# A two-layer attention model on one core: the rope of the keys done in place in the projection's PSUM bank, and their high and low parts taken from there

## The chip, the core and the metric

The kernel runs on one core of a Trainium2 chip. Its time is that of one execution on the device in microseconds (us). The engines are PE (TensorE matmuls; PEld is its weight load), DVE (VectorE), ACT (ScalarE), POOL (GpSimd) and SP (SyncE, which issues the DMAs). L211 is line 211 of the kernel before.

## The reference

512 tokens of width 1024 pass two layers. Each adds an attention and a feed forward with a causal convolution, each behind an RMS norm. Layer 0's attention (16 query heads, 4 key-value groups of width 64) has three branches with gates: compressed keys, selected blocks, and a window. Layer 1 (2 key-value groups) attends within a band of 128 tokens with a sink. Where keys are concerned, cut:

```python
def rope(x, pos):
    ...
    x1, x2 = xf[..., :half], xf[..., half:]
    return jnp.concatenate([x1 * cos - x2 * sin, x2 * cos + x1 * sin], axis=-1)

# layer 0
q, kc, vc, ks, vs, kw, vw, gl = jnp.split(h @ w_in, split_idx, axis=-1)
ks = rope(ks.reshape(b, s, g_n, dh), pos)
kw = rope(kw.reshape(b, s, g_n, dh), pos)
# layer 1
k, v = jnp.split(rms_norm(h, kv_norm) @ w_kv, 2, axis=-1)
k = rope(k.reshape(b, s, B_KV_HEADS, HEAD_DIM), jnp.arange(s))
```

All is float32.

## The kernel before

Every float32 product is made as three matmuls of rounded parts: x is hi + lo, and hi*hi, hi*lo and lo*hi are summed (mm3, L102 to L104). So each operand is copied to its high part on ACT and the low part is subtracted on DVE or POOL; for weights that is wh (L116) and wl (L117), and the strings W_A and W_B say weight by weight which of DVE and POOL subtracts. SPLIT_A and SPLIT_B say it for other operands by a key; 'kcat' stands for the low part of the keys.

The tokens are four tiles of 128. The PSUM banks are in three pools: pss (two tiles of two banks), pst (three of one bank) and psv (one). A projection to 256 columns of keys and values puts, for one token tile, two heads of keys (128 columns) beside two of values (128 columns). It comes out of project_steps, a pst tile per token tile (groups 1 to 3 of layer 0), or project_outer, all four token tiles in the two banks of one pss tile (group 0, and layer 1).

evac_kv takes such a token tile away. rope multiplies the keys by the cosines (L211, rope1) and the swapped halves by the sines (L214, rope2, two instructions) on DVE, from PSUM to SBUF, and sums the two (L215) to the SBUF tile kn. split_v scales the values and splits them from PSUM: high part on ACT (L268), low part on DVE (L269), both into Vg (VB in layer 1). cat_k copies kn to its high part on ACT (L198) and subtracts for the low part (L199), on DVE in layer 0 and on POOL in layer 1, into kcat. stack_k, called later, transposes kcat on PE (L282) to a pst tile, which ACT copies to Kg (KB in layer 1; L287). Queries take another way: rope to Qg or Qb (L211, L214, the sum L215 on DVE or POOL), a scaled copy qd on POOL (L291), transposes on PE (L300), then qh on ACT (L302) and ql on DVE (L303).

The attention goes by quads, four heads of a token tile: scores on PE into pss (L713, L714), their maximum nmx on DVE (L725), exponentials on ACT (L736), the gates prm or prl on POOL (L743), transposes (L310) to pth (ACT, L314) and ptl (DVE, L315), products with Vg into psv (L764, L765), then otmp on ACT (L327) and the sums osum on DVE (L331). The projections of the next group run among the quads of a group: weave and place put their steps at places given by tables, and a scheduler then sets the order of instructions on each engine by their dependences. Two engines that touch one PSUM bank are kept in order by semaphores, by bank, whichever columns they touch.

Of the kernel before, what the change touches and what calls it, by code (L numbers as in the profile page):

```python
# [33 lines left out]
# which of Pool (P) and DVE (V) takes a subtraction or sum that either can: the low parts of the weights, in  # L34
# order (layer 0, layer 1), and of other operands
W_A = "VVPVVVVVPPPPPPPPPVVVPPVVVVVPVVVVPPPPPPPPPPPVPPPVPVPPPPPPPPP"
W_B = "PVVVPVPVVPVPVPPVPPPPPPPPPPPPPPPPPPPPPPPP"
SPLIT_A = {'out': 'P', 'rope': 'S', 'ropek': 'V', 'kcat': 'V', 'cmp': 'V', 'stack': 'P', 'every': 99}
SPLIT_B = {'out': 'P', 'rope': 'S', 'kcat': 'P', 'stack': 'P'}
# where the steps of the attention phases go among one another, in units of quads (four heads of a token tile)  # L40
# [10 lines left out]
# where the norm of the first half of the tokens goes in the products of the second half  # L51
# [4 lines left out]
# columns of the constant table  # L56
# [5 lines left out]
# columns of the mask table  # L62
# [10 lines left out]
def hybrid_kernel(ctx, tc, t):  # L73
# [73 lines left out]
    def warm_exp(dep):  # L147
        # the exponential's table, loaded ahead of its first use
        act(small.tile([P, 1], F32, name="warm", bufs=1), dep, AF.Exp, scale=0.0)

# [12 lines left out]
    def token_scale(ssq=None):  # L163
        """1 / rms of each token, [P, NT] with tokens on partitions."""
# [10 lines left out]
    def spread_scale(r_nat):  # L175
        """The same along the free axis, on every partition, in PSUM."""
# [11 lines left out]
    def weave(*lists):  # L188
        """Emit lists of steps side by side, each in its own order; (steps, first, last) places one."""
# [28 lines left out]
    # in four steps, one token tile and one bank each  # L218
# [22 lines left out]
    # or in four steps along the contraction, two token tiles to a bank  # L241
# [19 lines left out]

    def rope_tables(r_nat, tab):
        for i in range(NT):
            nc.vector.tensor_scalar(tab[:, i], rope_t[:, i], r_nat[:, i:i + 1], None, op0=OP.mult)

    def split_v(dst, src, r):
        # dst [P, g, 2, 64] f32r, src [P, g, 64] in PSUM
# [4 lines left out]
    def cat_k(pool, k, n):  # L272
        # k [P, n, 64] natural -> the same as hi|lo
# [4 lines left out]
    def stack_k(dst, kc, n):  # L278
        # -> dst [(hi|lo, d), n, P]
# [26 lines left out]
    def probs_t(pool, blocks, way="V"):  # L306
        # four [P, P] blocks -> split [key, head, query]
# [851 lines left out]
```

## Time and profile before

| | |
|---|---|
| runs, median | 1300.07 us (1298.43 to 1300.89, 3 runs) |
| the profiled execution's own time: its span | 1298.1 us |
| PE busy | 1251.8 us, 96% |
| DVE busy | 831.9 us, 64% |
| ACT busy | 629.9 us, 49% |
| POOL busy | 661.4 us, 51% |

Busy shares are over the whole span: layer 0's attention takes about the first 350 us, layer 1's lies between about 750 and 900 us, and the rest is the feed forwards. An engine's idle time matters only where PE waits for it. A row's duration includes time in which an instruction is held back.

### The profile page before, as it was taken

The numbers are of one execution on the slowest core, as the hardware profiler recorded it, in microseconds if no ns is written. First come the engines' busy times: TensorE is split into PE (matmuls) and PEld (weight loads), VectorE is DVE, ScalarE is ACT, GpSimd is POOL, SyncE is SP. The second block draws the span as 40 slices with busy tenths as digits, with TensorE's granted clock in tenths as the row PEclk, the third lists the DMA queues.
The fourth block names the chain that finished last, engine by engine and source line by source line (L and its number), as shares of the span: only waits on it lengthen the run. The fifth ranks groups of instructions, "written<-read, shape, count | busy, mean of one in ns | idle before, by whom it ended". The sixth has DMA issues, their size and how long they took to land.

```text
span 1298.1 us, 17657 instructions
## 1 busy us (share of the span) xinstructions
PE 1251.8 (96%) x6539; PEld 1041.9 (80%) x6539; DVE 831.9 (64%) x1331; ACT 629.9 (49%) x1278; POOL 661.4 (51%) x536
## 2 busy tenths in 40 slices
PE   8988999999999999999999999899999999999997
PEld 7887787878778888888888898777788888888886
DVE  5877868787458775047776458775497730577712
ACT  4555867777454443124444347665454421344332
POOL 6425767766484444444445446664644444444452
PEclk9998999999999999999999999999999999999999
DMA  5342011121122222222222131111222222232221
GB/s 187 115 155 80 1 34 34 34 98 34 33 97 91 88 97 98 97 88 91 98 98 97 49 115 33 34 65 49 98 82 98 98 97 95 84 97 98 97 82 65
DMA packets 34085, 106.45 MB, mean 82 GB/s; under 512 B 4048, under 2 KB 6608, under 8 KB 34000
## 3 DMA queue, kind: packets, MB, share of 16 engines
q1 hardware_dynamic: 34000, 105.34, 24.1%
q8 instruction: 51, 0.84, 0.3%
q14 instruction: 34, 0.28, 0.1%
HBM read 103.23 MB, written 2.10 MB: 81 GB/s over the span
## 4 chain that ended last, share of the span: by engine, by line
PE 86%; DVE 8%; ACT 3%; issue 1%; DMA 1%; SPq 0%; POOL 0%; DVEq 0%; ACTq 0%; POOLq 0%
PE pss L103 14%; PE pss L104 14%; PE pss L102 14%; PE pst L102 10%; PE pst L104 10%; PE pst L103 10%; PE pst L310 3%; DVE s L185 2%; PE psv L765 1%; PE pss L713 1%; PE psv L764 1%; PE pss L714 1%; PE pst L300 1%; DVE s L347 1%; DVE nmx L725 1%
## 5 line engine op out<-in xcount | busy, mean ns | idle before, releaser
L117 POOL TENSOR_TENSOR wl<-wr,wh 128x1024 fp32r<-128x1024 f32 (+1 forms) x173 | 406.3, 2350 | 437.8 <-ACT wh L116 434.5
L116 ACT CAST wh<-wr 128x1024 fp32r<-128x1024 f32 (+2 forms) x201 | 197.7, 985 | 347.6 <-issue 173.1
L103 PE MATMUL pss<-s,wh 128*128 128x512 f32 x736 | 292.0, 397 | 3.8 <-DVE s L185 3.8
L102 PE MATMUL pss<-s,wh 128*128 128x512 f32 x736 | 291.3, 396 | 2.3 <-ACT s L198 2.1
L104 PE MATMUL pss<-s,wl 128*128 128x512 f32 x736 | 290.8, 396 | 0.0
L103 PEld LDWEIGHTS pss<-s,wh 128*128 128x128 f32 x736 | 138.3, 188 | 39.5 <-DVE s L185 6.2
L102 PEld LDWEIGHTS pss<-s,wh 128*128 128x128 f32 x736 | 138.1, 188 | 37.1 <-ACT s L198 3.0
L104 PEld LDWEIGHTS pss<-s,wl 128*128 128x128 f32 x736 | 138.3, 188 | 32.6
L104 PE MATMUL pst<-actv,wl 128*128 128x512 f32 (+1 forms) x363 | 141.0, 389 | 0.0
L103 PE MATMUL pst<-actv,wh 128*128 128x512 f32 (+1 forms) x363 | 140.7, 388 | 0.0
L102 PE MATMUL pst<-actv,wh 128*128 128x512 f32 (+1 forms) x363 | 140.3, 386 | 0.0
L415 DVE SCALAR_TENSOR_TENSOR cv<-u,convp,cv 128x512 f32<-128x512 f32 x88 | 123.2, 1439 | 13.4 <-ACT cv L414 13.4
L199 DVE TENSOR_TENSOR actv<-sa,actv 128x512 fp32r<-128x512 f32 x44 | 101.6, 2312 | 30.7 <-ACT actv L198 30.5
L443 DVE TENSOR_TENSOR s<-s,pst 128x512 f32<-128x512 f32 x31 | 21.3, 687 | 155.4 <-PE pst L104 155.4
L412 DVE TENSOR_TENSOR u<-pss,R 128x512 f32<-128x512 f32 x84 | 54.1, 686 | 64.5 <-PE pss L104 64.5
L420 ACT ACTIVATE sa<-cv 128x512 f32<-128x512 f32 x44 | 27.9, 634 | 123.1 <-DVE cv L417 123.0
L103 PEld LDWEIGHTS pst<-actv,wh 128*128 128x128 f32 x363 | 68.4, 188 | 15.2
L102 PEld LDWEIGHTS pst<-actv,wh 128*128 128x128 f32 x363 | 68.4, 188 | 14.8
L104 PEld LDWEIGHTS pst<-actv,wl 128*128 128x128 f32 x363 | 68.4, 188 | 13.9
L314 ACT CAST pth<-pst 128x512 fp32r<-128x512 f32 x92 | 53.7, 594 | 35.0 <-PE pst L310 30.9
L315 DVE TENSOR_TENSOR ptl<-pst,pth 128x512 fp32r<-128x512 f32 x92 | 62.2, 683 | 12.8 <-ACT pth L314 11.9
L414 ACT ACTIVATE cv<-u,convp 128x512 f32<-128x512 f32 x88 | 66.6, 807 | 2.2 <-DVE u L412 2.2
(242 smaller groups left out, 2634.4 us busy)
## 6 DMA issues: line engine op xcount, KB each, us to landing
wr<-fin SPq DMA_DIRECT2D x88, 512.0 KB, 3.3
wr<-fout SPq DMA_DIRECT2D x44, 512.0 KB, 3.2
wr<-wg SPq DMA_DIRECT2D x10, 512.0 KB, 3.3
wr<-cw SPq DMA_DIRECT2D x8, 512.0 KB, 3.4
wr<-woA SPq DMA_DIRECT2D x8, 512.0 KB, 3.8
wr<-woB SPq DMA_DIRECT2D x8, 512.0 KB, 3.3
wr<-wqb SPq DMA_DIRECT2D x6, 512.0 KB, 3.3
s<-xT SPq DMA_DIRECT2D x8, 256.0 KB, 5.3
```

Of the source, the lines that this page charges most:

```text
L102: mm(out, ah, bh, start=start, stop=False)
L103: mm(out, ah, bl, start=False, stop=False)
L104: mm(out, al, bh, start=False, stop=stop)
L116: nc.scalar.copy(hi[:, :n], raw[:, :n])
L117: engines[next(pick["w"], "P")].tensor_sub(lo[:, :n], raw[:, :n], hi[:, :n].bitcast(F32))
L199: engines[pick["split"][name] if name else "V"].tensor_sub(lo, src, hi.bitcast(F32))
L310: pe_tr(ps[:, r * P:(r + 1) * P], blocks[r], ident)
L314: nc.scalar.copy(ph, ps)
L315: nc.vector.tensor_sub(pl, ps, ph.bitcast(F32))
L412: nc.vector.tensor_mul(u[:, s, 2:], src, norm["R"])
L414: act(cv[:, s], u[:, s, 2:], AF.Identity, bias=par[:, 3:4], scale=par[:, 2:3])
L415: nc.vector.scalar_tensor_tensor(cv[:, s], u[:, s, 1:S + 1], par[:, 1:2], cv[:, s], op0=OP.mult, op1=OP.add)
```

## The change

rope_in_place multiplies the swapped halves by the sines into the SBUF tile rope2, then multiplies the keys by the cosines in place, PSUM to the same PSUM, and adds rope2 to them, again in place. cat_k then reads the keys from PSUM, on ACT and on DVE, and only after it split_v takes the values. The tile kn and the key 'ropek' go; in layer 1 'kcat' moves from POOL to DVE. The queries keep rope. The rest of the diff takes comments away.

```diff
-SPLIT_A = {'out': 'P', 'rope': 'S', 'ropek': 'V', 'kcat': 'V', 'cmp': 'V', 'stack': 'P', 'every': 99}
-SPLIT_B = {'out': 'P', 'rope': 'S', 'kcat': 'P', 'stack': 'P'}
+SPLIT_A = {'out': 'P', 'rope': 'S', 'kcat': 'V', 'cmp': 'V', 'stack': 'P', 'every': 99}
+SPLIT_B = {'out': 'P', 'rope': 'S', 'kcat': 'V', 'stack': 'P'}
...
+    def rope_in_place(pool, src, tab, n):
+        t2 = pool.tile([P, n, HD], F32, name="rope2", bufs=2)
+        for a, b in ((0, HALF), (HALF, 0)):
+            ss = tab[:, 1, a:a + HALF].unsqueeze(1).to_broadcast([P, n, HALF])
+            nc.vector.tensor_mul(t2[:, :, a:a + HALF], src[:, :, b:b + HALF], ss)
+        nc.vector.tensor_mul(src, src, tab[:, 0, :].unsqueeze(1).to_broadcast([P, n, HD]))
+        nc.vector.tensor_add(src, src, t2)
...
         def evac_kv(g):
             def evac(i, ps):
-                kn = pa.tile([P, 2, HD], F32, name="kn", bufs=2)
                 pv = ps[:, :256].rearrange("p (h d) -> p h d", d=HD)
-                rope(pa, kn, pv[:, 0:2], tab[:, i], 2, pick["split"]["ropek"] if g else "V")
+                rope_in_place(pa, pv[:, 0:2], tab[:, i], 2)
+                kcs[g, i] = cat_k(pa, pv[:, 0:2], 2)
                 split_v(V[g][:, i], pv[:, 2:4], r_nat[:, i:i + 1])
-                kcs[g, i] = cat_k(pa, kn, 2)
             return evac
...
         def evac_kv(i, ps):
-            kn = pb.tile([P, GB, HD], F32, name="kn", bufs=2)
             pv = ps.rearrange("p (h d) -> p h d", d=HD)
-            rope(pb, kn, pv[:, 0:GB], tab[:, i], GB)
+            rope_in_place(pb, pv[:, 0:GB], tab[:, i], GB)
+            kcs[i] = cat_k(pb, pv[:, 0:GB], GB)
             split_v(VB[:, i], pv[:, GB:2 * GB], r_nat[:, i:i + 1])
-            kcs[i] = cat_k(pb, kn, GB)
```

With the code the scheduler's order changes, in the two attentions alone. The changed kernel's line numbers are other ones: L267 is the half products, L268 the product in place, L269 the sum in place, L277 and L278 the values' parts, L291 stack_k's transposes, L296 its copy; L309, L311 and L312 are what L300, L302 and L303 were, L733, L340 and L747 what L725, L331 and L739 were.

First, DVE at the last key tile of layer 0's group 3, around 260 us in the trace of before. Before:

```order
L211 TENSOR_TENSOR rope_3497<-pst,tab 128x128
L214 TENSOR_TENSOR rope_3498<-pst,tab 128x2x32 x2
L215 TENSOR_TENSOR kn<-rope_3497,rope_3498 128x128
L269 SCALAR_TENSOR_TENSOR Vg<-pst,r_nat,Vg 128x2x64
L725 TENSOR_REDUCE nmx<-pss 128x2
L199 TENSOR_TENSOR kcat<-kn,kcat 128x2x64
L331 TENSOR_TENSOR osum<-psv,otmp 64x256 x2
```

The same stretch of DVE with the change:

```order
L267 TENSOR_TENSOR rope_3466<-pst,tab 128x2x32 x2
L268 TENSOR_TENSOR pst<-pst,tab 128x128
L269 TENSOR_TENSOR pst<-pst,rope_3466 128x128
L733 TENSOR_REDUCE nmx<-pss 128x2
L340 TENSOR_TENSOR osum<-psv,otmp 64x256 x2
L199 TENSOR_TENSOR kcat<-pst,kcat 128x2x64
L733 TENSOR_REDUCE nmx<-pss 128x2
L747 RECIPROCAL cf<-sums 128x2
L278 SCALAR_TENSOR_TENSOR Vg<-pst,r_nat,Vg 128x2x64
```

The low part kcat stands behind osum instead of ahead of it, and the values' low part Vg moves from the third place behind the products to the end.

Second, ACT where group 0's keys are put away at the start of the attention, around 91 to 97 us in the trace of before (prm is here a tile of the compression, ACT_TABLE_LOAD brings the table of the exponential). Before:

```order
L198 CAST kcat<-kn 128x2x64
L287 CAST KcT<-pst 128x128
L198 CAST kcat<-kn 128x2x64
L287 CAST Kg<-pst 128x256
L595 ACTIVATE prm<-psv 128x256
L116 CAST wh<-wr 128x1024
L149 ACT_TABLE_LOAD
L149 ACTIVATE warm<-prm 128x1
L287 CAST Kg<-pst 128x256
L302 CAST qh<-pst 128x512
L287 CAST Kg<-pst 128x256
```

The same stretch of ACT with the change:

```order
L277 ACTIVATE Vg<-pss,r_nat 128x2x64
L603 ACTIVATE prm<-psv 128x256
L116 CAST wh<-wr 128x1024
L149 ACT_TABLE_LOAD
L149 ACTIVATE warm<-prm 128x1
L296 CAST Kg<-pst 128x256
L198 CAST kcat<-pss 128x2x64
L311 CAST qh<-pst 128x512
L116 CAST wh<-wr 128x1024
L277 ACTIVATE Vg<-pss,r_nat 128x2x64
L296 CAST Kg<-pst 128x256
```

The last kcat of group 0 and the Vg behind it stand behind the table load; before, both kcat stood ahead of it.

Third, DVE at the start of layer 1's attention, around 758 to 769 us in the trace of before (rope<-pst and rope<-pss of 128x256 are queries, those of 128x128 keys). Before:

```order
L215 TENSOR_TENSOR kn<-rope_7538,rope_7539 128x128
L117 TENSOR_TENSOR wl<-wr,wh 128x1024
L269 SCALAR_TENSOR_TENSOR VB<-pss,r_nat,VB 128x2x64
L211 TENSOR_TENSOR rope_7556<-pss,tab 128x256
L214 TENSOR_TENSOR rope_7557<-pss,tab 128x4x32 x2
L215 TENSOR_TENSOR Qb<-rope_7556,rope_7557 128x256
L117 TENSOR_TENSOR wl<-wr,wh 128x1024
L211 TENSOR_TENSOR rope_7600<-pst,tab 128x256
L214 TENSOR_TENSOR rope_7601<-pst,tab 128x4x32 x2
L211 TENSOR_TENSOR rope_7610<-pss,tab 128x256
L214 TENSOR_TENSOR rope_7611<-pss,tab 128x4x32 x2
L215 TENSOR_TENSOR Qb<-rope_7610,rope_7611 128x256
```

The same stretch of DVE in layer 1 with the change:

```order
L199 TENSOR_TENSOR kcat<-pss,kcat 128x2x64
L211 TENSOR_TENSOR rope_7560<-pst,tab 128x256
L278 SCALAR_TENSOR_TENSOR VB<-pss,r_nat,VB 128x2x64
L267 TENSOR_TENSOR rope_7499<-pss,tab 128x2x32 x2
L214 TENSOR_TENSOR rope_7517<-pss,tab 128x4x32 x2
L268 TENSOR_TENSOR pss<-pss,tab 128x128
L215 TENSOR_TENSOR Qb<-rope_7516,rope_7517 128x256
L269 TENSOR_TENSOR pss<-pss,rope_7499 128x128
L214 TENSOR_TENSOR rope_7561<-pst,tab 128x4x32 x2
L211 TENSOR_TENSOR rope_7570<-pss,tab 128x256
L214 TENSOR_TENSOR rope_7571<-pss,tab 128x4x32 x2
L199 TENSOR_TENSOR kcat<-pss,kcat 128x2x64
```

Before, the last VB stands ahead of all query products. Now the query product out of pst stands ahead of the third VB, and the fourth token tile's rope and kcat lie among the queries' products.

## Rows read from the trace of the kernel before

**Rows 1.** The page, part 1: busy time of each engine, its share of the span, and its instructions.

```profile
PE 1251.8 (96%) x6539; PEld 1041.9 (80%) x6539; DVE 831.9 (64%) x1331; ACT 629.9 (49%) x1278; POOL 661.4 (51%) x536
```

**Rows 2.** The waits of PE over the whole span: tile and line that waited, engine, tile and line waited for, then microseconds in total, times, longest.

```profile
PE pst L282 <- DVE kcat L199: 3.9, 2, 2.1
...
PE pst L102 <- ACT Kg L287: 1.8, 2, 1.5
```

**Rows 3.** The view of the tile kn: duration in ns as min/median/max, then first and last start. L215 is the rope's sum, L199 the low part.

```profile
L215 DVE TENSOR_TENSOR kn<-rope,rope x20: 271/292/1878, 74.1 to 759.4; 128x128 f32<-128x128 f32 x20
...
L199 DVE TENSOR_TENSOR kcat<-kn,kcat x16: 266/289/2167, 75.9 to 263.6; 128x128 fp32r<-128x128 f32 x16
L199 POOL TENSOR_TENSOR kcat<-kn,kcat x4: 461/486/1367, 755.8 to 766.2; 128x128 fp32r<-128x128 f32 x4
```

**Rows 4.** Groups of instructions by line, with shapes kept apart: count, busy microseconds in all, mean ns of one, idle time before them. L211 and L214 are the products of the rope of one token tile's keys, L269 and L268 the two parts of its values.

```profile
L214 DVE TENSOR_TENSOR rope<-pst,tab 128x64 f32<-128x64 f32 x24 | 4.1, 214 | 0.0
...
L269 DVE SCALAR_TENSOR_TENSOR Vg<-pst,r_nat,Vg 128x128 fp32r<-128x128 f32 x12 | 4.1, 341 | 0.5 <-ACT Vg L268 0.4
...
L211 DVE TENSOR_TENSOR rope<-pst,tab 128x128 f32<-128x128 f32 x12 | 3.5, 288 | 5.0 <-PE pst L104 4.4 <-POOL wl L117 0.5
...
L268 ACT ACTIVATE Vg<-pst,r_nat 128x128 fp32r<-128x128 f32 x12 | 4.6, 382 | 7.1 <-DVE rope L214 7.1
```

**Rows 5.** The timeline around 200 us (last key tile of group 2), one row each of POOL, DVE and PE: start us, duration us (of all that a row counts together), engine, line, operation, tiles, count, and in brackets the idle time before it and what ended it. So are the columns in all groups from here on, but for the window in rows 6.

```profile
197.30 4.75 POOL L117 TENSOR_TENSOR wl<-wr,wh 128x1024 fp32r<-128x1024 f32 x2
...
200.02 2.17 DVE L199 TENSOR_TENSOR kcat<-kn,kcat 128x128 fp32r<-128x128 f32 x1
...
202.25 0.37 PE L282 MATMUL pst<-identr,kcat 128*128 128x128 f32 x2 [2.09 <-DVE kcat L199]
```

**Rows 6.** The timeline around 262 us (last key tile of group 3), of POOL, DVE, ACT and PE, and under it the window from 250 to 275 us: its length, busy time and instructions of PE, PEld, DVE, ACT and POOL, the granted clock of PE, the share of DMA, GB/s.

```profile
259.76 4.77 POOL L117 TENSOR_TENSOR wl<-wr,wh 128x1024 fp32r<-128x1024 f32 x2 [2.02 <-ACT wh L116]
...
260.62 1.69 DVE L215 TENSOR_TENSOR kn<-rope,rope 128x128 f32<-128x128 f32 x1
...
262.50 1.21 DVE L725 TENSOR_REDUCE nmx<-pss 128x2 f32<-128x1024 f32 x1
263.63 1.05 DVE L199 TENSOR_TENSOR kcat<-kn,kcat 128x128 fp32r<-128x128 f32 x1
264.60 0.84 DVE L331 TENSOR_TENSOR osum<-psv,otmp 64x256 f32<-64x256 f32 x2
...
262.94 0.58 ACT L327 COPY otmp<-psv 64x512 f32<-64x512 f32 x1
...
264.83 0.33 PE L282 MATMUL pst<-identr,kcat 128*128 128x128 f32 x2 [1.84 <-DVE kcat L199]
...
250.00:275.00 25.00, 22.40 (x149) 18.89 (x148) 20.26 (x45) 20.27 (x55) 18.11 (x20) 0.93 0.34 127
```

**Rows 7.** The timeline from 94 to 106 us (keys of group 0 put away, keys of group 1 projected), of ACT, DVE and PE.

```profile
94.74 1.28 ACT L149 ACT_TABLE_LOAD   x1
...
96.14 0.35 ACT L287 CAST Kg<-pst 128x256 fp32r<-128x256 f32 x1
...
100.32 0.37 ACT L268 ACTIVATE Vg<-pst,r_nat 128x128 fp32r<-128x128 f32 x1 [2.11 <-DVE rope L214]
...
99.88 0.34 DVE L214 TENSOR_TENSOR rope<-pst,tab 128x64 f32<-128x64 f32 x2
...
105.35 0.34 DVE L269 SCALAR_TENSOR_TENSOR Vg<-pst,r_nat,Vg 128x128 fp32r<-128x128 f32 x1
...
96.55 0.39 PE L102 MATMUL pst<-wh,s 128*128 128x256 f32 x1 [1.46 <-ACT Kg L287]
...
105.74 1.12 PE L300 MATMUL pst<-cst,qd 128*128 128x128 f32 x4 [0.81 <-DVE Vg L269]
```

**Rows 8.** The timeline from 766 to 770 us (start of layer 1's attention), of DVE, POOL and PE.

```profile
766.85 0.42 DVE L211 TENSOR_TENSOR rope<-pst,tab 128x256 f32<-128x256 f32 x1 [0.94 <-PE pst L104]
767.19 0.48 DVE L214 TENSOR_TENSOR rope<-pst,tab 128x128 f32<-128x128 f32 x2
767.58 0.41 DVE L211 TENSOR_TENSOR rope<-pss,tab 128x256 f32<-128x256 f32 x1
...
768.43 0.43 DVE L215 TENSOR_TENSOR Qb<-rope,rope 128x256 f32<-128x256 f32 x1
...
768.95 0.62 POOL L291 TENSOR_SCALAR qd<-Qb 128x512 f32<-128x512 f32 x1 [0.47 <-DVE Qb L215]
...
769.61 0.29 PE L282 MATMUL pst<-identr,kcat 128*128 128x128 f32 x2
769.74 0.62 PE L300 MATMUL pst<-cst,qd 128*128 128x128 f32 x4
```

**Rows 9.** The timeline around 111 and 249 us, of PE and DVE: the last matmul into the bank of a token tile, the last reader of that bank, and PE's next tile from the same pool.

```profile
110.85 0.28 PE L104 MATMUL pst<-wh,s 128*128 128x256 f32 x1
...
112.69 0.34 DVE L269 SCALAR_TENSOR_TENSOR Vg<-pst,r_nat,Vg 128x128 fp32r<-128x128 f32 x1
...
113.27 0.22 PE L671 MATMUL pst<-masks 128*128 128x128 bf16 x1
...
249.06 0.34 DVE L269 SCALAR_TENSOR_TENSOR Vg<-pst,r_nat,Vg 128x128 fp32r<-128x128 f32 x1
...
250.07 0.60 PE L310 MATMUL pst<-cst,prl 128*128 128x128 f32 x4
```

## The prediction

> **What bounds the kernel now.** Read the busy times first: PE works 1251.8 of 1298.1 us [rows 1], so at most 46 us of the span are PE's idle time, and the other engines, at 49 to 64%, matter only where PE waits for them. So the second view is PE's waits [rows 2]. One of them belongs to the code that changes: the transposes of stack_k wait 3.9 us, in two places, for the low part of the keys. A second wait, 1.8 us for the copy Kg, is the return of a PSUM bank. Third, the tile view shows what makes the low part late [rows 3]: the sum kn and the subtraction kcat last 0.29 us as a median and up to 1.88 and 2.17. Last, the timeline at the two places [rows 5, 6]. Around 200 us POOL subtracts two weight tiles from 197.30 to 202.05; DVE's kcat starts at 200.02, lasts 2.17 and ends just behind them, and PE's transpose follows after 2.09 us of waiting. Around 262 us another pair runs on POOL from 259.76 to 264.53; kn takes 1.69 and kcat 1.05 inside it, and PE waits 1.84. The values' low part (Vg, L269) has its source in PSUM and needs 341 ns as a mean of twelve [rows 4], with no such case. So a sum or difference of two SBUF tiles on DVE is held back while POOL subtracts SBUF tiles.
>
> The span is the profiled execution's own time; the median of the runs, 1300.07, is 2.0 above it. I sum against the span and add 2.0.
>
> **What the change removes.** Per token tile one 128x128 tile of SBUF traffic goes: kn is not written, and both the sum and the subtraction now have one operand in PSUM. DVE's instructions stay five per tile in layer 0 (two half products, product, sum, low part), on the same elements; in layer 1 the low part comes to them from POOL. No row shows DVE writing PSUM. The nearest rows: the product that reads PSUM and writes SBUF takes 288 ns, the half product 214 [rows 4], the sum that only touches SBUF 292 as a median [rows 3]. So reading PSUM costs nothing to speak of; I take 0.28 for each in-place instruction, the row it is nearest to. Bounds: 0.27 (the shortest SBUF sum), and double, 0.57, if the write back to PSUM doesn't overlap the read. The Trainium skill, Perfetto Trace Analysis, section Optimizing Scalar/DVE Operations, speaks against the change here: it gives DVE an overhead of about 60 ns on SBUF and 125 ns on PSUM, by which sum and low part would be some 65 ns dearer each, an estimate of 0.13 us per tile and of 0.65 us at the five places below; the rows named, 288 against 292, do not show it.
>
> The gain is the held-back time where PE waits for it. Around 200 us kcat shrinks from 2.17 to 0.28, and nothing else is late there: **-2.1** (the row's wait is 2.09). Around 262 us kn (1.69) and kcat (1.05) both shrink, but kcat stays behind nmx and, after the change, stands behind the two sums osum as well (0.84), which wait for ACT's copy otmp. Kn gives 1.41, kcat 0.77, osum takes 0.84 back: 1.34 in all, of which I leave some 0.25 for the wait on otmp: **-1.1**. Bounds: 0 (otmp ends at 263.52 as before, osum at 264.36, kcat at 264.64, PE starts at 264.8) and -1.84. The window around it ran at a granted clock of 0.93 [rows 6], so 14% of it, 3.5 us, at the lower of the two levels (1.2 instead of 2.4 GHz), which costs 1.75; PE had been idle before. As a wait remains, I count no gain there, and 1.75 as the far bound.
>
> **What it adds: a longer hold on each bank.** Keys and values of a token tile share a bank. ACT's Vg waits for DVE's rope products although it reads other columns (Vg at 100.32 starts 0.10 after the half products that ended at 100.22 [rows 7]; 7.1 us of such idle time in all [rows 4]): two engines do not touch a bank together in this program. Before, the bank was done with after products, Vg on ACT, Vg on DVE; sum, high and low part of the keys went on in SBUF. Now the bank goes DVE (products, sum), ACT (high), DVE (low), ACT (Vg), DVE (Vg). That adds a sum, 0.20 from start to start (its 0.28, of which 0.08 lies beside the next), a high part of 0.30, a low part of 0.28 and two hand-overs of 0.10: about **1.0 us more** until the bank comes back, at every token tile. Only where PE next wants the bank does it show. Two places [rows 9]: at 111 us the last reader ends at 113.03 and PE takes its next tile of the pool at 113.27, so 0.24 us of slack, **+0.75**; at 249 us it ends at 249.40 and PE comes at 250.07, slack 0.67, **+0.35**. Bounds for this term: 0, as the scheduler moves other matmuls ahead, and +4, if four or five more of the twelve tiles of groups 1 to 3 come late.
>
> At the start of attention [rows 7] two tiles are worse off. ACT's order now has the high part of group 0's last key tile behind the table load of 1.28 us at 94.74 (it stood before it). Kg is copied at 96.14, the high part follows at 96.39 and takes 0.30, the low part ends near 97.0, and PE's transposes take until 97.3, where before it went on at 96.55: **+0.75**. At 105.74 PE already waited 0.81 us for this bank (Vg ended at 105.69); the hold is 1.0 longer but the chain now starts behind fewer DVE instructions, so I take half: **+0.55**. Bounds for both: 0 and +2.
>
> Layer 1 [rows 8] has all four token tiles in the two banks of one pss tile. Before, ropes and VB of all four were done ahead of the queries; POOL made the low parts (0.49 each [rows 3]) off the path. Now DVE makes them, and DVE's order puts the products of the queries in the pst bank, which wait for PE until 766.85, ahead of the third tile's values and the whole of the fourth tile. From there, each at its duration less the 0.08 by which neighbours on DVE overlap (766.85 to 767.19 for a product of 0.42): that product 0.34, VB 0.26, half products 0.26, the queries' half products 0.39, product 0.20, Qb's sum 0.34, the keys' sum 0.20, another two half products 0.39, product 0.33, half products 0.39. That is 3.10; kcat starts at 769.95 and ends at 770.23, then Qb ends at 770.6 (it ended at 768.86), and POOL's qd, 0.62, at 771.3. PE wanted the transposes of kcat at 769.61 and those of qd at 769.74; it gets the second at 771.45: **+1.7**. Queued behind the waiting product are the remaining ropes, and for them PE. Bounds: 0, if PE reaches that place late, and +3.
>
> **Sum.** -2.1 - 1.1 + 0.75 + 0.35 + 0.75 + 0.55 + 1.7 = +0.9; span 1299.0, median about **1301.0**. The change moves waits, it does not remove them; elsewhere PE is the bound.
>
> **The rivals.** Faster: the stalls go whole and the new chains are hidden. For it: the two waits of 3.9 us are the only ones that PE has on these lines, and DVE is idle for a third of the span, so the 1.0 us may find room. Against: layer 1's order. With -3.9, the 1.75 at the lower clock, and layer 1's +1.7 the time is 1296.1; without the last, 1294.4. The Trainium skill, SBUF — State Buffer, section Who interferes with whom, says that a DVE instruction with two SBUF inputs contends with a GpSimd instruction that reads SBUF, and one with at most one SBUF input, outside the two-port modes, doesn't. By that rule all stretched kcat and kn go; the trace agrees as far as it shows it (2.17 beside a POOL pair of 4.75, nmx unharmed). Chance 0.22.
>
> Slower: the bank's hold decides. Its point is a slack under 1.0 us before PE's next tile of the three-bank pool; if half of the nine other tiles have none, that is 4.5 us at 1.0 each, and +5.4 with the sum: 1305.5. If the in-place write costs the double, 0.28 more on two instructions at each late place, eight to ten places, gives about the same, +5. For it: the waits for Kg and Vg at 96.55 and 105.74. Against: 1.8 and 0.81 us are all that the rows show of PE waiting for such banks. Chance 0.24.
>
> Nothing: both effects are absorbed, the gain by PE's next wait and the longer holds by slack, with PE at 96% anyway: 1300.1. Chance 0.12.
>
> **How the numbers follow.** The forecast has 0.42, its own range 1298.5 to 1304. A measurement of this kernel can tell about 0.2% (2.6 us) from no change, so 1297.5 to 1302.7 is the same. The forecast gives 0.30 to the same and 0.12 to slower; with the rivals faster is 0.22, the same 0.42, slower 0.36. The range 1296.3 to 1305.5 leaves about one in ten at each end.
>
> **What the profile of the changed kernel would show.** No wait of the transposes for kcat above 0.3 us near 202, and one shortened near 264; kcat on DVE at 0.27 to 0.30 with no stretched case; the in-place product and sum near 0.28; ACT's high part waiting for DVE at nearly every token tile; Vg's last reader about 1.0 us later after PE's last matmul; PE waiting some 1.7 us for qd near 770. Wrong if in-place instructions take 0.4 or more, if stretched ones remain, or if layer 1's qd is not late.

## The result, and the profile after

The changed kernel takes 1309.2 us (median of 4 runs, 1306.8 to 1310.3), the kernel before beside it 1299.5 (4 runs, 1298.4 to 1300.9): a ratio of 1.0076, interval 1.0062 to 1.009. It is 9.7 us slower, where 1301.0 was forecast and a range up to 1305.5. The profiled execution's span is 1307.5 us, 9.4 above that of before.

The page, part 1, of the changed kernel, for [rows 1]:

```profile
PE 1253.5 (96%) x6539; PEld 1040.0 (80%) x6539; DVE 831.4 (64%) x1335; ACT 628.7 (48%) x1278; POOL 657.1 (50%) x532
```

The other engines work as long as before or less. PE, with the same 6539 instructions, is busy 1.7 us longer; the other 7.7 of the 9.4 us are its idle time. Its waits over the whole span, for [rows 2]:

```profile
PE pst L319 <- POOL prb L961: 4.6, 1, 4.6
PE pst L291 <- DVE kcat L199: 4.3, 3, 2.2
...
PE psv L772 <- ACT pcb L737: 2.1, 1, 2.1
...
PE pst L319 <- DVE pcb L689: 0.8, 1, 0.8
```

The wait for kcat is not gone: 3.9 us in two places became 4.3 in three. The first and the third are new or grown: before, the longest wait for POOL's prb was 1.5 us, and there was none for pcb on psv. The last one shrank: it was 2.5 before. The view of the tile kcat, and of lines L268 and L269 (ns as min/median/max), for [rows 3]:

```profile
L199 DVE TENSOR_TENSOR kcat<-pst,kcat x12: 277/290/293, 102.1 to 266.9; 128x128 fp32r<-128x128 f32 x12
...
L199 DVE TENSOR_TENSOR kcat<-pss,kcat x8: 277/284/292, 75.2 to 772.8; 128x128 fp32r<-128x128 f32 x8
...
L199 DVE TENSOR_TENSOR kcat<-prm,kcat x1: 1862/1862/1862, 87.1 to 87.1; 128x64 fp32r<-128x64 f32 x1
...
L268 DVE TENSOR_TENSOR pst<-pst,tab x12: 285/299/300, 101.1 to 264.0; 128x128 f32<-128x128 f32 x12
...
L269 DVE TENSOR_TENSOR pst<-pst,rope x12: 285/299/300, 101.4 to 264.3; 128x128 f32<-128x128 f32 x12
```

All twenty low parts of the keys take 277 to 293 ns, none is held back, and the two in-place instructions take 0.30 us. (The one of 1862 ns is the compression's, of two SBUF tiles, which the change leaves as it was; PE does not wait for it.) What the change was costed at, instruction by instruction, came true; the loss lies in what waits for what.

To place it I compare when PE comes to the same instruction in both traces: its products of probabilities with values (160 in layer 0, 56 in layer 1 in either). The table gives how much later, in us, for the change and for the kernels of the experiments, at the products that stand at 150, 310, 786 and 845 us in before. One execution is good to 1 or 2 us, as layer 0's columns of the l1 kernels show, which leave that layer as it was.

```
                 150    310    786    845
change          -1.8   +2.9   +7.4   +9.4
l0_only         -1.5   +4.4   +4.4   +4.4
l1_only          0.0   +1.0   +5.4   +7.3
before_swapped  +0.3   -0.2   -0.2   +0.3
l1_kcat_dve     -0.2   -0.7   -0.7   -0.1
l1_recip        +0.3   -0.5   +3.2   +4.9
l1_both         -0.9   -1.4   +5.1   +6.7
sum_out         -4.3    0.0   -0.1   +0.7
v_first         -0.5   +3.6   +6.6   +6.7
l0_hold         -0.7   +6.7   +6.6   +6.7
l0_hi_dve       -4.4   +0.4   +0.4   +0.4
l1_hi_dve       -0.6   -1.1   +0.1   +0.2
l1_nocoll       +1.9   +1.5   +7.9   +6.3
g01_chain       -2.7   -1.2   -1.2   -0.6
g23_chain       -0.4   +6.7   +6.7   +6.8
g01_hi_dve      -5.8   -6.8   -6.8   -5.8
hi_dve          -3.8   -0.5   +0.7   +0.8
g0_hi_dve       -3.1   -2.3   -2.3   -1.4
g01_last        -4.6   -7.6   -7.6   -7.0
```

The change gains 1.8 us until 150 us (groups 0 and 1 are put away there), loses 4.7 from there to 310 (groups 2 and 3), and 6.5 in layer 1.

**Groups 2 and 3.** The timeline from 245 to 254 us, the second key tile of group 3; columns as in rows 5. L268 and L269 are the product and the sum, L733 and L736 maxima of scores, L336 takes the attention's output, L324 the low part of the transposed probabilities, L772 the product with the values:

```profile
246.65 0.28 PE L104 MATMUL pst<-wh,s 128*128 128x256 f32 x1
...
247.57 0.29 DVE L268 TENSOR_TENSOR pst<-pst,tab 128x128 f32<-128x128 f32 x1
247.96 0.96 DVE L733 TENSOR_REDUCE nmx<-pss 128x2 f32<-128x768 f32 x1
248.83 0.29 DVE L269 TENSOR_TENSOR pst<-pst,rope 128x128 f32<-128x128 f32 x1
...
249.21 0.27 ACT L198 CAST kcat<-pst 128x128 fp32r<-128x128 f32 x1 [2.46 <-DVE cmx L736]
...
250.09 0.28 DVE L199 TENSOR_TENSOR kcat<-pst,kcat 128x128 fp32r<-128x128 f32 x1
...
251.18 0.58 ACT L336 COPY otmp<-psv 64x512 f32<-64x512 f32 x1
251.79 0.59 ACT L323 CAST pth<-pst 128x512 fp32r<-128x512 f32 x1
...
252.68 0.69 DVE L324 TENSOR_TENSOR ptl<-pst,pth 128x512 fp32r<-128x512 f32 x1
252.79 0.47 PE L772 MATMUL psv<-pth,Vg 128*128 128x512 f32 x1 [2.06 <-ACT pcb L737]
253.10 0.38 ACT L277 ACTIVATE Vg<-pst,r_nat 128x128 fp32r<-128x128 f32 x1
...
253.42 0.38 PE L102 MATMUL pst<-wh,s 128*128 128x256 f32 x1 [0.16 <-DVE ptl L324]
253.57 0.34 DVE L278 SCALAR_TENSOR_TENSOR Vg<-pst,r_nat,Vg 128x128 fp32r<-128x128 f32 x1
```

The last matmul ends at 246.93, the last reader of the bank at 253.91: it is held for 6.98 us, where before the same tile, its last matmul ending at 246.97, gave it back at 249.40 after 2.43 [rows 9]. Each step that a hand-over opens stands in its engine's queue: a reduction of 0.96 between product and sum, another ahead of the low part, and on ACT otmp, pth and exponentials ahead of Vg. PE's next token tile starts at 253.42, when the copies of the transposes let go of the pool's next bank; before, that tile ran from 251.05 to 254.12, and now PE waits 2.06 us on L772 with nothing to put there. Over the twelve tiles of groups 1 to 3 the mean hold, from the last matmul's end to the last reader's, went from 2.75 to 4.8 us, over groups 2 and 3 from 2.4 to 4.7. Of the 4.7 us lost, 1.8 fall in group 2, though its wait of 2.09 is gone, and 2.9 in group 3: at the product that stands at 242 us in before the lag is 0.0.

**The last tile of group 3**, for [rows 6]:

```profile
263.27 0.28 PE L104 MATMUL pst<-wh,s 128*128 128x256 f32 x1
...
264.67 0.58 ACT L336 COPY otmp<-psv 64x512 f32<-64x512 f32 x1
...
266.01 0.84 DVE L340 TENSOR_TENSOR osum<-psv,otmp 64x256 f32<-64x256 f32 x2
...
266.88 0.29 DVE L199 TENSOR_TENSOR kcat<-pst,kcat 128x128 fp32r<-128x128 f32 x1
...
267.31 0.34 PE L291 MATMUL pst<-identr,kcat 128*128 128x128 f32 x2 [1.48 <-DVE kcat L199]
```

The same tile's last matmul in the kernel before:

```profile
259.71 0.28 PE L104 MATMUL pst<-wh,s 128*128 128x256 f32 x1
```

kcat takes 0.29 and no longer 1.05, but it stands behind osum, as the order said. It ends 3.6 us behind the tile's last matmul, where before it ended 4.7 behind it [rows 6]; PE, whose order is another too, begins to wait 2.3 us behind that matmul and not 3.0. So the wait shrank from 1.84 to 1.48 only.

**Layer 1.** First the two places of the forecast, for [rows 8]; then the first quad's softmax: mxb the maximum, esb and denb the denominator, L954 its reciprocal, prb the probabilities that POOL scales (L961) and PE transposes (L319). Under it two windows with the granted clock (the number behind POOL's count), and two short ones cut out of them:

```profile
773.20 0.34 PE L291 MATMUL pst<-identr,kcat 128*128 128x128 f32 x2 [0.56 <-DVE kcat L199]
...
774.16 0.66 PE L309 MATMUL pst<-cst,qd 128*128 128x128 f32 x4 [0.61 <-POOL qd L300]
...
779.04 1.23 DVE L946 TENSOR_REDUCE mxb<-pss 128x4 f32<-128x1024 f32 x1 [0.52 <-PE pss L936]
...
783.72 0.23 ACT L952 ACTIVATE esb<-esb 128x4 f32<-128x4 f32 x1
...
784.66 2.35 POOL L117 TENSOR_TENSOR wl<-wr,wh 128x1024 fp32r<-128x1024 f32 x1
...
785.27 1.77 DVE L953 TENSOR_TENSOR denb<-denb,esb 128x4 f32<-128x4 f32 x1
786.96 1.21 DVE L117 TENSOR_TENSOR wl<-wr,wh 128x1024 fp32r<-128x1024 f32 x1
...
788.17 1.21 DVE L946 TENSOR_REDUCE mxb<-pss 128x4 f32<-128x1024 f32 x1
...
789.30 0.16 DVE L954 RECIPROCAL denb<-denb 128x4 f32<-128x4 f32 x1
...
790.11 0.69 PE L319 MATMUL pst<-cst,prb 128*128 128x128 f32 x2 [4.62 <-POOL prb L961]
...
765.00:790.00 25.00, 19.32 (x158) 18.37 (x157) 19.33 (x53) 10.95 (x30) 11.06 (x12) 0.96 0.20 63
790.00:815.00 25.00, 24.35 (x166) 21.96 (x167) 17.30 (x41) 15.33 (x48) 14.63 (x30) 0.90 0.09 36
788.10:790.11 2.01, 0.00 (x0) 0.00 (x1) 1.65 (x7) 1.77 (x8) 0.54 (x2) 0.51 0.39 124
790.11:795.00 4.89, 4.89 (x19) 4.06 (x20) 2.77 (x7) 3.73 (x15) 4.89 (x11) 0.50 0.42 167
```

The same softmax and the first two windows of the kernel before (L946 and L947 are denb and its reciprocal there):

```profile
775.28 1.23 DVE L939 TENSOR_REDUCE mxb<-pss 128x4 f32<-128x1024 f32 x1
...
780.01 0.21 ACT L945 ACTIVATE esb<-esb 128x4 f32<-128x4 f32 x1
...
780.82 0.15 DVE L946 TENSOR_TENSOR denb<-denb,esb 128x4 f32<-128x4 f32 x1
...
781.59 0.17 DVE L947 RECIPROCAL denb<-denb 128x4 f32<-128x4 f32 x1
...
783.27 0.44 PE L310 MATMUL pst<-cst,prb 128*128 128x128 f32 x2 [1.54 <-POOL prb L954]
...
765.00:790.00 25.00, 22.60 (x179) 21.09 (x178) 18.94 (x50) 13.83 (x45) 16.20 (x24) 1.00 0.26 85
790.00:815.00 25.00, 24.57 (x188) 22.31 (x187) 20.24 (x46) 18.64 (x53) 14.57 (x26) 1.00 0.00 1
```

From esb to the reciprocal it was 1.6 us and is 5.6. DVE's order there is another: a weight's low part and a third maximum stand ahead of the reciprocal, and the tiny addition denb, two SBUF operands, lasts 1.77 us beside POOL's wl, not 0.15. PE's wait grew by 3.1 us.

At a clock of 0.96 and 0.90, 8% and 20% of the two windows, 7.0 us, ran at 1.2 and not 2.4 GHz. That did not cost half of 7.0: the first 2.0 of them lie in the wait, where PE has no matmul, and the 4.9 behind it are the stretch that PE worked through at the lower clock. The lag of the change, place by place, is 2.9 us at the end of layer 0, 3.8 when PE comes to the wait for prb, 6.8 when that wait is over, 8.5 at the products around 806 us, 9.4 at those from 830 on, behind a second stretch at the lower clock that is longer than before's (granted clock 0.90 and not 0.95 from 815 to 850 us). So, by the unrounded lags, the 6.5 of the table are 0.8 before the wait, 3.1 in it, 1.6 behind it and 0.9 around 825 us.

### The profile page after: what moved, and what is told of

Same layout as the page of the kernel before. It is cut to its first block, busy times and chain, and to the rows that moved or that the text cites. A ratio compares the mean times of both kernels' runs of the same rounds, so it can differ in the third digit from the quotient of the medians.

```text
span 1307.5 us, 17640 instructions
## 1 busy us (share of the span) xinstructions
PE 1253.5 (96%) x6539; PEld 1040.0 (80%) x6539; DVE 831.4 (64%) x1335; ACT 628.7 (48%) x1278; POOL 657.1 (50%) x532
## 4 chain that ended last, share of the span: by engine, by line
PE 84%; DVE 9%; ACT 3%; issue 2%; DMA 1%; POOL 0%; SPq 0%; DVEq 0%; ACTq 0%; POOLq 0%
PE pss L103 14%; PE pss L104 14%; PE pss L102 14%; PE pst L102 10%; PE pst L104 10%; PE pst L103 10%; PE pst L319 3%; DVE s L185 2%; PE psv L773 1%; PE pss L721 1%; PE psv L772 1%; PE pss L722 1%; DVE nmx L733 1%; DVE wl L117 1%; PE pst L309 1%
## 5 line engine op out<-in xcount | busy, mean ns | idle before, releaser
L199 DVE TENSOR_TENSOR actv<-sa,actv 128x512 fp32r<-128x512 f32 x44 | 101.6, 2312 | 30.7 <-ACT actv L198 30.6
L324 DVE TENSOR_TENSOR ptl<-pst,pth 128x512 fp32r<-128x512 f32 x92 | 62.5, 684 | 14.6 <-ACT pth L323 13.7
```

The source lines that it names most:

```text
L199: engines[pick["split"][name] if name else "V"].tensor_sub(lo, src, hi.bitcast(F32))
L324: nc.vector.tensor_sub(pl, ps, ph.bitcast(F32))
```

## The experiments

The kernel before, beside which each set ran, had medians from 1298.9 to 1300.0. Ratios are to it, with 95% intervals. "The change in layer 0" stands for the diff's first evac_kv, "in layer 1" for the second with SPLIT_B.

### Which layer

```diff
 # l0_only: the change in layer 0; layer 1 as before
 # l1_only: the change in layer 1; layer 0 as before
 # l1_kcat_dve: before, and
-SPLIT_B = {'out': 'P', 'rope': 'S', 'kcat': 'P', 'stack': 'P'}
+SPLIT_B = {'out': 'P', 'rope': 'S', 'kcat': 'V', 'stack': 'P'}
 # before_swapped: before, and in both evac_kv
-                split_v(V[g][:, i], pv[:, 2:4], r_nat[:, i:i + 1])
                 kcs[g, i] = cat_k(pa, kn, 2)
+                split_v(V[g][:, i], pv[:, 2:4], r_nat[:, i:i + 1])
```

> In place in layer 0 alone; layer 1 as before. PE's progress in the changed kernel lags by 3.0 us at the end of layer 0's attention and by 9.5 at the end of layer 1's. If the two layers are independent, this kernel is 3.0 us slower than before (2 to 4). If layer 0's loss only comes from something that layer 1 shares, it is within 1 us of before.

Measured 1302.9, ratio 1.0033 (1.002 to 1.0046).

> In place in layer 1 alone; layer 0 as before. Independent layers: 6.4 us slower than before (5.5 to 7.5). My first working gave 1.7 for layer 1; the rest would then be the wait of 4.6 us for the gates of the first quad (prb on POOL), which stands behind a reciprocal that DVE's order now has behind a weight's low part and the next maxima. If that wait is a matter of where layer 0 ends, it is gone here and the loss is 1.5 to 2.5.

Measured 1306.6, ratio 1.0061 (1.0043 to 1.008), with the wait of 4.6 us for prb and clocks of 0.93 and 0.94 in the two windows. Both layers lose by themselves, each somewhat more than expected. Their sum is 0.94% and the change's own loss 0.76%; the difference is within the noise of the two runs.

> The kernel before with one letter changed: layer 1's low part of the keys on DVE instead of POOL, out of SBUF as before. Theory: the loss of layer 1 comes from the shared bank's chain and from the order that follows from it, not from DVE's four more subtractions: within 1 us of before. Rival: DVE's added work in that place is the cause: 3 us or more slower.

Measured 1300.1, ratio 1.001 (1.0 to 1.0019). That DVE makes layer 1's low part, from SBUF as here, is not the cause.

> The kernel before with the two calls exchanged, the keys' parts taken ahead of the values' parts, still out of kn in SBUF. No chain in a bank is longer for it, and layer 1's order of instructions on DVE stays as before; layer 0's order changes a little. Theory that the loss is the longer chain in the bank: within 1 us of before. Rival that any change of the scheduler's order costs some us, whatever the chain: 2 to 4 us slower.

Measured 1299.5, ratio 1.0008 (0.9999 to 1.0017). Nor is the order of values and keys in the code, as long as the keys' parts come from SBUF.

### Layer 1: the reciprocal, the queries, the collision

```diff
 # l1_recip: l1_only, and the first quads' reciprocals keep their place on DVE
+                    first.append(nc.vector.reciprocal(den, den))
...
+        with tc.issue_after(first[0].ins) if first else ExitStack():
             eng.tensor_sub(lo[:, :n], raw[:, :n], hi[:, :n].bitcast(F32))
 # l1_both: l1_recip, and the queries' ropes behind the last VB
+                with tc.issue_after(lastv[0].ins):
                     rope(pb, Q[q][:, i], ps.rearrange("p (h d) -> p h d", d=HD), tab[:, i], 4, pick["split"]["rope"] if q else "V")
 # l1_nocoll: l1_only, and one letter of W_B (the weight that collides) is V instead of P
```

> In place in layer 1 alone, as in the run before, and in DVE's order the reciprocal of the first quad's sums is kept ahead of the low part of the next weight and of the third quad's maxima, where the kernel before has it. The chain of the keys is unchanged. In the run without this, PE waits 4.6 us for that quad's gates (1.5 in the kernel before), and its granted clock is 0.93 and 0.94 in the 50 us from 765 on. Theory: of layer 1's 6 to 7 us the keys' chain gives about 1.7 directly, and the rest comes from this place in DVE's order and from the lower clock that follows the wait: 2 to 3 us slower than before. Rival: the chain itself makes the first quads late, wherever the reciprocal stands: 5 us or more slower.

Measured 1304.6, ratio 1.0035 (1.0025 to 1.0046). The wait for prb fell from 4.6 to 0.5 us, and another came; waits of PE from 750 to 900 us:

```profile
PE pss L936 <- ACT prb L957: 4.8, 2, 3.7
```

The scores of a later quad now wait for a pss tile that ACT's exponentials still read. The place of the reciprocal is worth some 3 us of 8, with intervals that leave it between nothing and 6; the rest, between what theory and rival had said, stays wherever it stands.

> As the run with the reciprocal kept in place, and the products of the queries' rope are also kept behind the last value part of the keys' bank on DVE, as in the kernel before, so that no key tile stands behind a product that waits for PE. Theory: the keys' low part of the fourth tile and the first quad's queries come 1 to 1.7 us earlier, and the kernel is within 1.5 us of before. Rival: DVE then idles on the bank's hand-overs with the queries behind it, and the first quad's queries are as late as without it: 2 to 4 us slower.

Measured 1308.9, ratio 1.0068 (1.0053 to 1.0083), with a new wait of 3.1 us for POOL's qd: slower than either expectation. Keys first and queries behind them only moves the lateness to the queries.

> The change in layer 1 alone, and one weight's low part moved from POOL to DVE: the one beside which DVE's sum of the first quad (denb, 128x4) takes 1.77 us in the changed kernel. Theory: that collision, which the shifted time of the first quads brought about, is the larger part of layer 1's loss: PE's wait of 4.6 us falls below 2.5 and the kernel is 3 to 5 us slower than before instead of 7.6. Rival: the sum is late anyway, and DVE's added 1.2 us costs what the collision did: 6 us or more slower.

Measured 1306.5, ratio 1.0053 (1.0038 to 1.0069), the wait for prb still 4.2. denb takes 0.15 us now, but the weight's 1.22 stands on DVE ahead of it. So the collision can be taken away without a gain; what it costs by itself is not shown, since DVE got the weight's work in its place.

### How the bank is passed on

```diff
 # sum_out: in both layers product in place, but the sum leaves PSUM (out is kn); the rest as before
-        nc.vector.tensor_add(src, src, t2)
+        nc.vector.tensor_add(src if out is None else out, src, t2)
 # v_first: the whole change, split_v ahead of cat_k
 # l0_hold: before, and in layer 0 two instructions behind split_v, whose result nobody reads
+                nc.scalar.copy(pv[:, 0:2], pv[:, 0:2])
+                nc.vector.tensor_mul(pv[:, 0:2], pv[:, 0:2], tab[:, i, 0, :].unsqueeze(1).to_broadcast([P, 2, HD]))
 # l0_hi_dve, l1_hi_dve, hi_dve: the change in layer 0, in layer 1, in both, with the high part on DVE
-        split_sb(kc[:, :n, 0], kc[:, :n, 1], k, "kcat")
+        if dve:
+            nc.vector.tensor_copy(kc[:, :n, 0], k)
+            nc.vector.tensor_sub(kc[:, :n, 1], k, kc[:, :n, 0].bitcast(F32))
+        else:
+            split_sb(kc[:, :n, 0], kc[:, :n, 1], k, "kcat")
```

> Half of the change, in both layers: the product with the cosines in place in PSUM, but the sum written to kn in SBUF, and the keys' parts taken from there behind the values' parts as before (layer 1's low part on POOL). The bank has no more hand-overs between engines than before. DVE's order in layer 1 is that of before. Theory that the hand-overs in the bank cost the time: within 1.5 us of before, and kn no longer stretched beside POOL (0.29 instead of up to 1.88). Rival that writing PSUM in place costs it: 3 us or more slower.

Measured 1302.5, ratio 1.0027 (1.0015 to 1.0039), in runs from 1300.5 to 1307.4; the profiled one is the shortest. That is more than the theory of the hand-overs allows (1.5 us) and about what the rival said. The price of writing PSUM is not the reason, since the product in place takes 0.30 us here as in the change. The hold is 3.2 us as a mean, 2.7 in groups 2 and 3. Layer 1 loses nothing; layer 0 is 4.3 us ahead by 150 us and gives all of it back by 310.

> The whole change, but the values' parts taken ahead of the keys' parts. The bank is held as long as in the changed kernel, the keys come later by an ACT and a DVE instruction. Theory that the hold on the bank is what costs: 5 to 10 us slower than before, as the changed kernel. Rival that it is the values' parts being last which costs: 0 to 3 us slower.

Measured 1306.0, ratio 1.0044 (1.0029 to 1.006). Layer 1 costs 3.1 and not 6.5, layer 0 about the same; the hold is 4.9.

> The kernel before, and in layer 0 two instructions more on each token tile's bank, behind the values' parts: a copy of the keys' columns in place on ACT and a product in place on DVE, whose results nobody reads. The keys take their old way through kn. So the bank is held by one ACT and one DVE hand-over more, and nothing else waits for that. In the changed kernel the twelve banks of groups 1 to 3 are held 4.8 us as a mean against 2.75 before. Theory that the hold alone makes layer 0's 3 to 4 us: 2 to 5 us slower than before. Rival that it is the later keys (or the order of their parts) and not the bank: within 1.5 us of before.

Measured 1306.4, ratio 1.0054 (1.0039 to 1.007), hold 4.8. Two small instructions more on the bank, with values and keys as before, cost 7 us, more than expected, all between 150 and 310 us. A longer hold, with the order that the scheduler makes around it, is enough for a loss of that size there.

> The change in layer 0 alone, with the high part of the keys copied by DVE instead of ACT. The bank then passes DVE, ACT (values), DVE: as many hand-overs as before, and DVE does one 0.28 us copy more per tile. Theory that the hand-overs, each behind other work of the two engines, make the hold long: hold near 3.2 us as a mean and within 1.5 us of before (the run with the change in layer 0 alone was 4.0 slower). Rival that work on the keys in PSUM itself is slow: 3 us or more slower.

Measured 1298.9, ratio 1.0001 (0.9991 to 1.0012). The time came as expected but not for the reason given: the hold stayed at 4.7. This kernel is 4.4 us ahead by 150 us and loses 4.8 by 310.

> The change in layer 1 alone, with the high part of the keys copied by DVE instead of ACT; DVE's order behind the first quads is then that of before again. Theory: fewer hand-overs bring the four key tiles through the bank earlier, the sums of the first quad are not held beside a weight's low part on POOL, and the kernel is 0 to 2.5 us slower than before instead of 7.6. Rival: DVE's added copies make the first quads as late as the hand-overs did: 5 us or more slower.

Measured 1299.2, ratio 0.9997 (0.9988 to 1.0006); the wait for prb is 1.5 us as before, the clock 1.00 in both windows. In layer 1 the hand-over to ACT and back is the cause, with the order that follows from it.

> The whole change, in both layers, but with the high part of the keys made by DVE and not by ACT: two hand-overs of the bank fewer for each token tile. Layer 0 alone in this form stood at 1.0001 and layer 1 alone at 0.9997. If the extra hand-overs are the whole of the +9.7 us: within 1.5 us of before. Rival, the orders of the two layers depend on each other: 3 us or more above before.

Measured 1299.8, ratio 1.0008 (0.9997 to 1.0019). Without that hand-over the whole change costs nothing; its halves in layer 0 cancel.

### Which groups of layer 0

```diff
 # g01_chain: g in (0, 1); g23_chain: g in (2, 3); layer 1 as before
+                if g in (0, 1):
+                    rope_in_place(pa, pv[:, 0:2], tab[:, i], 2)
+                    kcs[g, i] = cat_k(pa, pv[:, 0:2], 2)
+                    split_v(V[g][:, i], pv[:, 2:4], r_nat[:, i:i + 1])
+                else:
...
 # g01_hi_dve, g0_hi_dve: g in (0, 1), g == 0, and the high part on DVE
 # g01_last: the same with
+                if g in (0, 1) or i == NT - 1:
```

> The change in layer 0 for the key-value groups 0 and 1 alone, ACT making the high part as in the change; groups 2 and 3 and layer 1 as before. If the loss of layer 0 comes from the longer hold of the banks in groups 2 and 3: PE is 0.5 to 2 us ahead of before by 150 us, keeps it to 310 us, and the time is 0.5 to 2 us under before (1297 to 1298.7). If the loss comes from the high part of the keys on ACT wherever it stands: PE loses as much as the layer-0 change alone did (it lost 4.4 by 290 us), at least half of it, so 1301 to 1303.

Measured 1299.9, ratio 1.0003 (0.9994 to 1.0011). Ahead by 2.7 us at 150 us; half of it is given back.

> The change in layer 0 for groups 2 and 3 alone, groups 0 and 1 and layer 1 as before. If the hold in groups 2 and 3 is the loss: nothing changes until 150 us, PE loses 4 to 6 us between 150 and 310 us, time 1303 to 1305, more than the layer-0 change as a whole (1302.9), which has the gain of the start in it. Rival, the start's chain is what costs: within 1.5 us of before, and the two collisions that this kernel removes (the waits of 2.09 and 1.84 us near 202 and 264 us) bring it 2 to 3 us under.

Measured 1305.8, ratio 1.0049 (1.0037 to 1.0062). The loss of layer 0 is in groups 2 and 3, and it is larger than that of the four groups together and than expected. PE's longest wait there is the one above at another time:

```profile
255.08 0.47 PE L778 MATMUL psv<-pth,Vg 128*128 128x512 f32 x1 [2.06 <-ACT pcb L743]
```

> Groups 0 and 1 alone, with DVE making the high part too, so that the bank goes DVE, ACT, DVE as before with the keys' parts ahead of the values'; groups 2 and 3 and layer 1 as before. The layer-0 change with this high part in all four groups was 4.7 us ahead at 150 us and lost 5 by 310 us. If both halves are separate: 3 to 5 us under before, 1294 to 1296, ratio 0.996 to 0.998. Rival, what is gained early is given back at the next thing that PE waits for (loads of weights, or the softmax of the first quads): within 1 us of before.

Measured 1294.5, ratio 0.9963 (0.9951 to 0.9975): faster than both kernels. PE's longest wait from 100 to 150 us and that window, in before, then the window in g01_hi_dve:

```profile
124.93 0.41 PE L310 MATMUL pst<-cst,prm 128*128 128x128 f32 x2 [2.46 <-DVE pcb L681]
...
100.00:150.00 50.00, 44.11 (x288) 36.42 (x288) 41.49 (x117) 37.21 (x122) 36.09 (x50) 0.93 0.13 43
```

```profile
100.00:150.00 50.00, 45.49 (x315) 36.82 (x313) 44.55 (x130) 40.79 (x141) 40.03 (x57) 1.00 0.10 33
```

The wait of 2.5 us for pcb at 124.9 us is gone, PE works 1.4 us more, and the clock stays at its upper level: at 0.93, 14% of the window, 7 us, ran at 1.2 GHz; PE worked all through them, so they cost 3.5 us by estimate. Yet the four tiles of group 1 hold their banks 4.9 us and not 3.4: here a longer hold does no harm. That PE wants the keys there and not the bank is my reading of it.

> The keys' parts in place and ahead of the values', high part on DVE, in layer 0's group 0 alone; groups 1 to 3 and layer 1 as before. If the gain of 5.5 us comes from the first group, whose keys the first quads of the attention wait for: 1294 to 1296. If group 1, whose tiles run beside those quads, makes it: within 1 us of before. Both in equal parts: about 1297.

Measured 1296.7, ratio 0.9977 (0.9968 to 0.9986): by difference, groups 0 and 1 share the gain about equally.

> Groups 0 and 1 in place with the high part on DVE, and of groups 2 and 3 the last token tile only, the one whose keys PE waits 2.08 and 1.84 us for near 196 and 259 us. If a tile gains where PE waits for its keys and loses where PE waits for its bank: the two waits go and the time is 2 to 3.5 us under that of groups 0 and 1 alone (1294.5), 1291 to 1292.5. Rival, every longer hold in groups 2 and 3 costs: these two tiles hold their bank 1.3 and 2.5 us longer as in the change, so the time is at or above 1294.5.

Measured 1292.9, ratio 0.9944 (0.9931 to 0.9957), the fastest. The two waits for kcat are gone although these two tiles hold their banks 4.9 and 5.3 us, 0.6 and 2.7 more than before. Behind these two no key tile of the same pool comes for some 40 us, or none at all, which would explain it.

## Why the prediction was wrong

**The stretched instructions: right.** No low part of the keys is held back, and the wait of 2.09 near 202 us is gone, as forecast. The rule of the Trainium skill (SBUF — State Buffer, Who interferes with whom) that one SBUF operand does not contend agrees with the 277 to 293 ns of all twenty; the two at 199.5 and 266.9 us ran beside a POOL subtraction of weights and took 291 and 292.

**The in-place price: right.** 0.30 us against 0.28 taken; the bound of 0.57 was far off. The 65 ns for PSUM that the forecast worked out from the Trainium skill (Perfetto Trace Analysis, Optimizing Scalar/DVE Operations) are not there: 299 ns for the sum against 292 [rows 3], 290 for the low part against 289.

**The place near 262 us: mis-sized.** -1.1 was forecast, -0.4 came. The low part itself came as priced, 1.1 us earlier behind its tile's last matmul. That PE, in its own new order, would want it 0.7 us earlier too was no term.

**The start: wrong sign in the end.** Forecast +0.75 and +0.55. PE goes on at the two places at 97.04 and 106.02, 0.5 and 0.3 later, and then gains: the place at 150 us is 1.8 us earlier. The first place, and the window from 100 to 150 us:

```profile
96.87 0.34 PE L291 MATMUL pst<-identr,kcat 128*128 128x128 f32 x2 [2.23 <-DVE kcat L199]
97.04 0.35 PE L102 MATMUL pst<-wh,s 128*128 128x256 f32 x1
...
100.00:150.00 50.00, 45.41 (x306) 36.76 (x305) 42.60 (x125) 38.77 (x131) 37.53 (x53) 0.97 0.13 43
```

The wait of 2.46 for pcb fell to 0.83 and the clock was 0.97, not 0.93. Neither was a term of the sum; what brought the quads forward is not shown.

**The bank's hold: the step that failed in layer 0.** "About 1.0 us more" counted a hand-over as 0.10 and the instruction behind it as if its engine were free. The hold grew by 2.1 us as a mean (2.3 in groups 2 and 3), since each hand-over joins a queue of reductions of 0.96 and exponentials of 0.6. And only two tiles were held to be late; between 150 and 310 us PE lost 4.7, with -2.5 of removed waits in it. The slower rival named this mechanism, with 1.0 a tile.

**Layer 1: the right place, and stopped there.** +1.7 at qd was forecast; the two waits of 0.56 and 0.61 came, and PE was 1.5 later there. The step that failed is that the sum ended at that row. What it sets off, the first softmax in another order with a wait of 4.6 us and the lower clock behind it, made it 6.5.

None of the prediction's three signs of being wrong came: they asked for the price in place, the stretching and a late qd. What failed stood in the list before them, the last reader 1.0 us later.

**What stays open.** How much of layer 0's loss is the hold itself and how much the order that the scheduler makes around it: sum_out, with a hold only 0.3 us longer in groups 2 and 3, also gave back 4.3 us between 150 and 310, and l0_hi_dve, with the hold of the change, lost as much. l0_hold shows that a longer hold can bring such a loss, g23_chain where it is; no run changes the hold with the order kept.

## What to carry to other kernels

Cost a resource that passes between engines by the queues behind each hand-over, not by the hand-over: look at what stands on the next engine at that place. With one engine for both parts the edit gained in groups 0 and 1 and at the last tiles, where PE had waited for the keys, and it lost in groups 2 and 3; with the high part on ACT it gained nothing in groups 0 and 1 (1.0003). Do it place by place. And follow a late instruction past the first engine that it stops, to the next softmax and the clock behind it.

## What the runs showed of the hardware

A product and a sum on DVE from PSUM into the same PSUM take 0.30 us for 128x128, as from SBUF. An addition of 128x4 elements in SBUF took 1.77 us beside a POOL subtraction of two SBUF tiles (2.35 us), 0.15 in the kernel before. A wait of PE can cost more than its length: at the end of the 4.6 us for prb the granted clock fell to 0.51 and 0.50 until 795 us, of which PE worked 4.9 us, and PE lost another 1.6 us; where that wait was 1.5, in before and in l1_hi_dve, the clock was 1.00 from 765 to 815 us. Time at the lower clock costs nothing while PE waits anyway: 2.0 us of it did here.
